# A two-layer trunk on one core: early splits of the weight blocks behind each norm, a shorter norm chain, a rebuilt opening and new ranks

## The chip, the core and the metric

The kernel runs on one core of a Trainium2 chip. PE (TensorE) multiplies, ACT (ScalarE) and DVE (VectorE) do the elementwise work, POOL (GpSimd) some fetches and stores, and SP (SyncE) issues most of the transfers from HBM. The metric is the device time of one execution in microseconds; the time before is the median of three runs, and one further execution was profiled.

## The reference, cut

```python
D_MODEL = 2048; SEQ = 256; DEPTH = 2; D_FF = 5120      # one sequence, f32
# layer 0: mixer = gated DeltaNet (16 q/k heads, 32 v heads of 128, chunks of 64)
# layer 1: mixer = sparse attention (16 heads of 128, an indexer picks the keys), bias by distance
for i in range(DEPTH):
    x = layer_norm(alpha * x + mixer_i(x), ln1_g[i], ln1_b[i])
    x = layer_norm(alpha * x + conv_glu(x), ln2_g[i], ln2_b[i])
    x = x + sigmoid(x @ ple_w_gate[i]) * (p[i] @ ple_w_proj[i])
...
def layer_norm(x, g, b):
    mu = jnp.mean(xf, -1, keepdims=True)
    var = jnp.mean(jnp.square(xf - mu), -1, keepdims=True)
    y = (xf - mu) * lax.rsqrt(var + LN_EPS) * g + b
```

So there are four norms: norm 1 and norm 2 in layer 0 (behind the mixer and behind the feed-forward part), norm 3 and norm 4 in layer 1.

## The kernel before

All 256 rows of x stay in the core (two tiles of 128 rows, called a = 0 and 1), and the weights, some 500 MB, are streamed once. A weight block is 128 x 1024 numbers, 512 KB. `weigh` makes three steps of it: a load into one of three `raw` buffers, issued by SP (L349); a rounded copy `hi`, by ACT (L354) or, when pressed, by DVE (L358); and `lo`, the rest `raw - hi`, by DVE (L362). hi and lo have three buffers each. PE then multiplies x, split in the same way and transposed (`xT`), by both: in wide blocks (mm_ps: L306 by hi, 512 columns, and L303 by lo, 256 columns) or in column blocks of 512 outputs (b_ps: L316 and L317 by hi, L319 by lo). A `column` is the chain of blocks that fills one pair of PSUM tiles; at its end `done` takes it on.

At a norm, `project` adds the product to x by a residual operation on DVE (L217 or, unscaled, L215) and takes statistics (L1102). `norm` aggregates them (L1111), works out 1/sqrt by `newton` (L628 to L643), subtracts and scales x (L1124 on DVE for a = 0, L1126 on ACT for a = 1, which needs `nm` of L1115), has PE transpose it (n_ps, L1134), applies gain and bias (L1145 on ACT, L1149 on DVE) and splits it (cast L1158, rest L1161, both on DVE). While that chain runs, PE has only the two `fill` columns of p @ ple_w_proj (b_ps<-hi,pT), two blocks in all. The first products behind a norm need the first pair of xT and the first blocks' hi and lo.

The order of the work is made ahead of time by a planner: `add(engine, estimated us, what, dependencies, rank=...)` puts a step on an engine, and of the steps that could start, the one of least rank goes first. `RANK` holds the numbers: 'later' is the rank of a weight split that is not yet pressing, 'near' says how many blocks ahead it becomes pressing. Each engine, and each queue of transfers, then runs its list in order.

The opening loads ident by SP (L197), x in quarters (L266), and the first blocks of gdn_w_in; POOL issues five small constants (L248 to L252). Layer 0's mixer ends with eight groups: `mixes(5)` and `mixes(6)` multiply groups' outputs by gdn_w_o and add them to x, and `project` does it for group 7 (O[7], written by L979, ready when `od[7]` is). In layer 1's mixer, `fetch` loads the bias tiles by POOL (L1408). The last columns of the second layer go through `ple`: sigmoid on ACT (L1296), product and sum on DVE (L1298, L1300), and the output's transfer (L1303).

## Time and profile before

| | us |
|---|---|
| median of 3 runs | 2812.58 (2812.26 to 2814.76) |
| the profiled execution, its own time | 2815.96 |
| its span | 2814.1 |
| PE busy in the span | 2787.2 |
| DVE busy | 1883.9 |
| ACT busy | 1420.6 |

The span is the time from the first to the last instruction of the profiled execution; 1.86 us of its time lie around it. Busy times are sums over an engine's instructions; weight loads of PE run beside its products. An idle time in the views is put down to the event that ended it.

### The profile page before, as it was taken

The numbers are of one execution on the slowest core, as the hardware profiler recorded it, in microseconds if no ns is written. First come the engines' busy times: TensorE is split into PE (matmuls) and PEld (weight loads), VectorE is DVE, ScalarE is ACT, GpSimd is POOL, SyncE is SP. The second block draws the span as 40 slices with busy tenths as digits, with TensorE's granted clock in tenths as the row PEclk, the third lists the DMA queues.
The fourth block names the chain that finished last, engine by engine and source line by source line (L and its number), as shares of the span: only waits on it lengthen the run. The fifth ranks groups of instructions, "written<-read, shape, count | busy, mean of one in ns | idle before, by whom it ended". The sixth has DMA issues, their size and how long they took to land.

```text
span 2814.1 us, 39810 instructions
## 1 busy us (share of the span) xinstructions
PE 2787.2 (99%) x15054; PEld 2405.8 (85%) x15054; DVE 1883.9 (67%) x2931; ACT 1420.6 (50%) x2260; POOL 115.1 (4%) x191
## 2 busy tenths in 40 slices
...
GB/s 190 216 187 162 180 153 189 169 155 166 159 139 167 206 206 210 207 197 189 187 200 191 197 208 174 183 152 159 191 173 195 199 196 189 198 192 186 198 181 190
DMA packets 402272, 519.62 MB, mean 185 GB/s; under 512 B 19708, under 2 KB 288384, under 8 KB 402080
## 3 DMA queue, kind: packets, MB, share of 16 engines
...
## 4 chain that ended last, share of the span: by engine, by line
PE 93%; DVE 3%; DMA 3%; ACT 1%; issue 0%; SPq 0%; ACTq 0%; DVEq 0%
PE mm_ps L306 32%; PE mm_ps L303 17%; PE b_ps L317 12%; PE b_ps L316 12%; PE b_ps L319 12%; PE s_ps L834 2%; DMA raw<-in_gdn_w_in 2%; DVE lo L362 1%; DMA raw<-in_dsa_w_in 1%; PE o_ps L940 1%; PE w_ps L834 0%; PE ss_ps L661 0%; PE sc_ps L1384 0%; PE lg_ps L1470 0%; ACT hi L354 0%
## 5 line engine op out<-in xcount | busy, mean ns | idle before, releaser
L362 DVE TENSOR_TENSOR lo<-raw,hi 128x1024 fp32r<-128x1024 f32 x925 | 1129.4, 1223 | 724.6 <-ACT hi L354 716.3
L354 ACT ACTIVATE hi<-raw 128x1024 fp32r<-128x1024 f32 (+1 forms) x878 | 928.6, 1058 | 1166.7 <-PE mm_ps L306 535.7
L306 PE MATMUL mm_ps<-xT,hi 128*128 128x512 f32 (+1 forms) x4176 | 1028.8, 395 | 6.3 <-ACT hi L354 3.7
L306 PEld LDWEIGHTS mm_ps<-xT,hi 128*128 128x128 f32 (+1 forms) x4176 | 764.5, 189 | 154.9 <-ACT hi L354 4.3
L303 PEld LDWEIGHTS mm_ps<-xT,lo 128*128 128x128 f32 (+1 forms) x4176 | 537.3, 191 | 22.4 <-DVE lo L362 2.0
L303 PE MATMUL mm_ps<-xT,lo 128*128 128x256 f32 (+1 forms) x4176 | 549.6, 284 | 1.4 <-DVE lo L362 1.3
L316 PE MATMUL b_ps<-hi,xT 128*128 128x512 f32 (+1 forms) x704 | 273.3, 390 | 3.9 <-DVE xT L1158 2.6
L317 PE MATMUL b_ps<-hi,xT 128*128 128x512 f32 (+1 forms) x704 | 270.7, 387 | 0.4 <-DVE xT L1161 0.4
L316 PE MATMUL b_ps<-hi,hTA 128*128 128x512 f32 x512 | 199.4, 389 | 0.0
L317 PE MATMUL b_ps<-hi,hTA 128*128 128x512 f32 x512 | 199.4, 389 | 0.0
L319 PE MATMUL b_ps<-lo,xT 128*128 128x512 f32 (+1 forms) x704 | 187.4, 387 | 0.0
L316 PEld LDWEIGHTS b_ps<-hi,xT 128*128 128x128 f32 x704 | 132.8, 189 | 30.3 <-DVE xT L1158 3.1
L317 PEld LDWEIGHTS b_ps<-hi,xT 128*128 128x128 f32 x704 | 132.9, 189 | 26.4 <-DVE xT L1161 1.1
L319 PEld LDWEIGHTS b_ps<-lo,xT 128*128 128x128 f32 x704 | 129.6, 189 | 25.8
L319 PE MATMUL b_ps<-lo,hTA 128*128 128x512 f32 x512 | 136.9, 390 | 0.0
L317 PEld LDWEIGHTS b_ps<-hi,hTA 128*128 128x128 f32 x512 | 96.2, 188 | 19.9
L316 PEld LDWEIGHTS b_ps<-hi,hTA 128*128 128x128 f32 x512 | 96.2, 188 | 19.9
L319 PEld LDWEIGHTS b_ps<-lo,hTA 128*128 128x128 f32 x512 | 96.2, 188 | 19.9
L316 PE MATMUL b_ps<-hi,oT 128*128 128x512 f32 x256 | 102.9, 402 | 0.0
L317 PE MATMUL b_ps<-hi,oT 128*128 128x512 f32 x256 | 100.3, 392 | 0.0
L445 DVE SCALAR_TENSOR_TENSOR ac<-pd,cw,ac 128x256 f32<-128x256 f32 x192 | 90.7, 481 | 3.7 <-ACT ac L442 0.4
L1228 DVE SCALAR_TENSOR_TENSOR fac<-fpd,fcw,fac 128x256 f32<-128x256 f32 x160 | 73.7, 481 | 2.8
(287 smaller groups left out, 2333.9 us busy)
## 6 DMA issues: line engine op xcount, KB each, us to landing
...
raw<-in_ffn_w_gate SPq DMA_DIRECT2D x160, 512.0 KB, 4.5
raw<-in_ffn_w_up SPq DMA_DIRECT2D x160, 512.0 KB, 3.7
raw<-in_ffn_w_down SPq DMA_DIRECT2D x160, 512.0 KB, 4.0
...
```

Of the source, the lines that this page charges most:

```text
L303: nc.tensor.matmul(ps[o][:m, S:], lo[:, k, o * P:o * P + m], xk[:, 0], start=False, stop=e)
L306: nc.tensor.matmul(ps[o][:m], hi[:, k, o * P:o * P + m], xk.rearrange("p a b -> p (a b)"), start=s, stop=e)
L316: nc.tensor.matmul(ps[o][:, c], xh, hi[:, k, c], start=s, stop=False)
L317: nc.tensor.matmul(ps[o][:, c], xl, hi[:, k, c], start=False, stop=False)
L319: nc.tensor.matmul(ps[o][:, c], xh, lo[:, k, c], start=False, stop=e and c.stop == n)
L354: nc.scalar.activation(hi, box["raw"], AF.Copy)
L362: nc.vector.tensor_tensor(lo, box["raw"], box["hi"].bitcast(F32), op=ALU.subtract)
L445: nc.vector.scalar_tensor_tensor(box["ac"], pd[:, k:k + S], wt[:, k:k + 1], box["ac"], op0=ALU.mult, op1=ALU.add)
L834: nc.tensor.matmul(ps[:, h], lhs[:, h], rhs[:, h], start=True, stop=True)
L940: nc.tensor.matmul(ps[:, h], qd()[:, a, h], u()[:, a, h], start=not a, stop=True)
L1228: x = add(V, 0.48, lambda k=k, pd=pd, ac=ac, m=m: nc.vector.scalar_tensor_tensor(ac(), pd()[:, k:k + S], w["taps"](k, m), ac(), op0=ALU.mu ...
```

## The change

The change has six parts.

- **Opening.** ident is loaded by ACT's queue, and the five constants by SP, behind the third to sixth weight block (`settings`). The first quarter of x and the first two weight blocks are loaded and split in halves. Six products of zeros (`spin`) run on PE before the first real product.
- **Early splits.** `weigh` takes a `home`: blocks that are used behind a norm are loaded into the right half of `pw` and split into tiles that hold nothing at that time (hTB at norm 1; xT2 and hTB at norm 3; hTA at norms 2 and 4), while the last column of the projection runs: two fill blocks at norm 1, the two fills and the first four blocks behind the norm at the others. `after` puts the next five blocks' splits behind certain pairs of the norm.
- **Norm chain.** `newton` has 8 operations in place of 10, `nm` is made beside the chain, the first x piece of a = 1 is DVE's. The last column of a projection ends in three pieces (512, 256 and 256 wide), and `close` interleaves the last two blocks so that a = 0 ends first. `weave` takes the first gate and up blocks by halves.
- **Groups 6 and 7** are projected together, in one PSUM chain of 8 (`project` of gdn_w_o[24 * P:]); group 7's own steps get rank `last`, and its root is taken apart for each a.
- **Tail.** The last column of `ple` ends in pieces of 512, 256 and 256.
- **Queues and ranks.** The bias tiles are loaded by SP at rank -1 behind weight loads; the numbers of `RANK` change.

The diff, cut to its core:

```diff
-            'later': 3.45,
-            'cast': 2,
+            'later': 2.2,
...
-            'hold': 0.9}
+            'hold': 0.05,
...
-        nc.sync.dma_start(out=self.ident, in_=t["cst"][:, C_IDENT:C_IDENT + P])
+        nc.scalar.dma_start(out=self.ident, in_=t["cst"][:, C_IDENT:C_IDENT + P])
...
+        def spin(n, begin=False, end=False):
+            if begin:
+                box1["ps"] = sps("bk", [S], "w_ps")
+            for _ in range(n):
+                nc.tensor.matmul(box1["ps"], pads[0][:, :P], pads[0][:, 3:], start=True, stop=True)
+
+        spun = add(E, 5.0, lambda: spin(5, True), take=["bk"], rank=-9)
...
+            d = [order[2]["load"]]
+
+            def one():
+                nc.sync.dma_start(out=cr, in_=t["gdn_conv_w"].rearrange("k (n c) -> n k c", c=P))
+
+            def two():
+                for i, k in enumerate(("gdn_dt_bias", "gdn_a_log")):
+                    nc.sync.dma_start(out=w[:, 256 + 32 * i:288 + 32 * i],
+                                      in_=bass.AP(tensor=t[k].tensor, offset=t[k].offset, ap=[[0, P], [1, 32]]))
+
+            def three():
+                nc.sync.dma_start(out=ng, in_=t["gdn_norm_g"].rearrange("(p o) -> p o", o=1))
+                nc.sync.dma_start(out=self.cst, in_=t["cst"][:, P:])
+            a = add(Q, 0.4, one, behind=d, rank=2.2, bus=0.6, tail=2.0)
+            b = add(Q, 0.8, two, behind=[order[4]["load"]], rank=4.2, bus=0.2, tail=2.0)
+            return a, add(Q, 0.8, three, behind=[order[5]["load"]], rank=6.2, bus=1.1, tail=2.0), b
...
+            n = 2 if not nb else 4
+            for j in range(0, 4, n):
+                parts = []
+                k0 = 4 * nb + j
+                for a in range(2):
+                    def load(a=a, k0=k0):
+                        cs = slice(k0 * P, (k0 + n) * P)
+                        nc.sync.dma_start(out=self.x[:, a, cs], in_=t["x"][a * P:(a + 1) * P, cs])
...
+                    if a and not k0:
+                        add(E, 0.45, lambda: spin(1), [e], behind=[spun], give=["bk"], rank=0.5)
...
+                ends = [(0, slice(0, 512)), (1, slice(0, 256)), (1, slice(256, 512))] if split and k0 + nk == kt else None
...
+                raw = box["raw"] = (home(2).rearrange("p (k n) -> p k n", k=b["nk"]) if home else
+                                    self.wp.tile(shape, F32, tag="raw", name="raw"))
...
+                hi = box["hi"] = at_home(0) if home else self.hl.tile(shape, F32R, tag="hi", name="hi")
...
+            if i < 2:
+                h, l = [], []
+                for j in range(2):
+                    def load(j=j):
+                        (c0, n) = b["cols"]
+                        if not j:
...
+                    d = b["load"] = add(Q, 0.38, load, take=["raw"] * (not j), rank=i if i else j - 2.5, bus=0.9, tail=2.0,
+                                        behind=[d] if j else [last["load"]] if i else ())
+                    h.append(add(A, 0.63, high, [d], take=["hi"] * (not j), rank=0, behind=h[:j],
+                                 other=(V, 0.39, cast, lambda: 1)))
+                    l.append(add(V, 0.66, low, [h[j]], take=["lo"] * (not j), give=["raw"] * j, rank=0, behind=l[:j]))
...
+            if home is None:
+                behind, ahead = [*behind, *split[:1]], split[1:]
+            else:
+                ahead = ()
+            h = add(A, 0.2 + 0.86 * size, high, [d, *deps], take=["hi"] * (not home), rank=urgent, behind=behind,
                     other=(V, 0.1 + 0.6 * size, cast, lambda: R["cast"] if near() else 9))
-            l = add(V, 0.1 + 1.13 * size, low, [h], take=["lo"], give=["raw"], rank=urgent)
-            b["weights"] = dict(hi=h, lo=l)
+            l = add(V, 0.1 + 1.13 * size, low, [h], take=["lo"] * (not home), give=["raw"] * (not home), rank=urgent,
+                    behind=ahead)
...
+        def close(a, b):
+
+            weigh(a)
+            weigh(b)
+            ks, (one, *two) = range(2), b["ends"]
+            multiply(a, [(one, ks)], False)
+            multiply(b, [(one, ks)], False)
+            multiply(a, [((1, slice(0, 512)), ks)], True)
+            multiply(b, [(w, ks) for w in two], True)
+
+        def weave(a, b):
+
+            weigh(a)
+            weigh(b)
+            for j in (0, 2):
+                for one in (a, b):
+                    multiply(one, pieces(one, range(j, j + 2)), j == 2)
...
+        def after(blocks, pairs):
+
+            rest = [b for b in blocks if "weights" not in b]
+            for n, b in enumerate(rest[:5]):
+                k = R["after"] + n - R["free"]
+                weigh(b, behind=pairs[k][1:] if n >= R["free"] and k < 8 else ())
+
+        def run(blocks, soon=()):
+
+            for i, b in enumerate(blocks):
+                if i in soon:
+                    weigh(*soon[i]())
+                if "next" in b:
+                    return close(b, b["next"])
...
-            def step():
-                y, u, zz = box["y"], box["t"], z()
-                nc.vector.scalar_tensor_tensor(u, y, -0.5 / c, y, op0=ALU.mult, op1=ALU.mult)
-                nc.vector.tensor_tensor(u, u, zz, op=ALU.mult)
-                nc.vector.scalar_tensor_tensor(y, u, 1.5, y, op0=ALU.add, op1=ALU.mult)
...
+                nc.vector.tensor_scalar(yi, yi, -1.0, 1595561664.0, op0=ALU.mult, op1=ALU.add)
+
+            def more(ks):
+                y, u = box["y"], box["t"]
+                if ks[0][0] == 3:
+                    nc.vector.tensor_tensor(u, y, y, op=ALU.mult)
+                    nc.vector.tensor_tensor(u, u, z(), op=ALU.mult)
+                    box["p"] = z()
+                for k, c in ks:
+                    nc.vector.scalar_tensor_tensor(box["p"] if k else y, box["p"] if k < 3 else u, c, u if k else y,
+                                                   op0=ALU.add, op1=ALU.mult)
...
+            v_ = R["last"] if last else 2
...
+            for aa in ((0,), (1,)) if last else ((0, 1),):
...
+                    for i, (a, c, w) in enumerate(spans(nb)):
+                        xs_ = self.x[:, a, nb * 512 + c:nb * 512 + c + w]
+                        d = add(V, 0.14 + 0.275 * w / 256, lambda a=a, c=c, w=w, xs_=xs_: self.residual(
+                            xs_, state["ps"][a][:, c:c + w], scale), [task[i] if nb == 3 else task],
+                            give=["mm"] * (c + w == 512), rank=-2 if nb == 3 else 1)
...
+            minus = add(V, 0.16, lambda: nc.vector.scalar_tensor_tensor(
+                nm(), mv()[:, 1, 0:1], -1.0, r()[:, 1:2], op0=ALU.mult, op1=ALU.mult), [d], rank=-1.5)
...
+                        if a and k0 and k0 < R["even"]:
+                            before.append(add(A, 0.37 + 0.112 * n, lambda xa=xa: nc.scalar.activation(
+                                xa, xa, AF.Identity, scale=r()[:, 1:2], bias=nm()), [minus], rank=rank, behind=held))
+                        else:
+                            before.append(add(V, 0.14 + 0.13 * n, even, [d], rank=rank if k0 else -1.7, behind=held if a else ()))
...
-                        r[a, h] = add(G, 0.75, lambda a=a, h=h: nc.gpsimd.dma_start(
+                        r[a, h] = add(Q, 0.5, lambda a=a, h=h: nc.sync.dma_start(
...
+                            [opened, *stored], behind=[gates[a * 4 + h // 4]], rank=-1, bus=1.2 + 1.2 * a, tail=4.0)
...
-            run(mixes(6))
...
-                    c, st, stat = project(t["gdn_w_o"][28 * P:], 4, lambda k: O[7]()[:, k], lambda k0: od[7], 1.0, opened)
-                run(two(c[0], c[1]) if i else c[0] + c[1])
-                run(c[2])
-                run(c[3])
+                    c, st, stat = project(t["gdn_w_o"][24 * P:], 8, lambda k: O[6 + k // 4]()[:, k % 4],
+                                          lambda k: od[6 + k // 4], 1.0, opened)
...
+                homes = [(w["hB"], 0), (w["hB"], 1)]
+                blocks = [fills[0], fills[1]]
+                if i:
+                    blocks += [first[0][0], first[1][0], first[0][1], first[1][1]]
+                    homes = [(xb2, m) for m in range(4)] + homes
+                    deps = [opened, seq[-1]["task"]]
+                else:
+                    deps = [opened]
+                c = two(c[0], c[1]) + c[2] + c[3] if i else c[0][:2] + c[1][:2] + c[0][2:] + c[1][2:] + c[2] + c[3]
+                run(c, ahead_(range(16, 28, 2) if i else (8, 10, 12), blocks, homes, lambda n, deps=deps: deps))
...
+                blocks = [fills[2], fills[3], g[0][0], g[1][0], g[0][1], g[1][1]]
+                run(x, ahead_(range(6, 18, 2), blocks, [(w["hA"], m) for m in range(6)],
+                              lambda n, x=x: [x[2 * n + 1]["task"]]))
```

How the order of the engines changes, at three places. On DVE at norm 3, from the end of newton on, the order before; L362 is the lo of a weight block, L1158 and L1161 are the first pairs of x:

```order
L642 TENSOR_TENSOR rt_18615<-rt_18615,lz 128x2
L643 SCALAR_TENSOR_TENSOR rs_18614<-rt_18615,rs_18614 128x2
L1115 SCALAR_TENSOR_TENSOR lnm<-lmv,rs_18614 128x1
L1124 TENSOR_SCALAR x<-x,lmv,rs_18614 128x256 x2
L362 TENSOR_TENSOR lo<-raw,hi 128x1024 x3
L1158 CAST xT<-xb 128x2x256
L1161 TENSOR_TENSOR xT<-xb,xT 128x2x256
L1158 CAST xT<-xb 128x2x256
L1161 TENSOR_TENSOR xT<-xb,xT 128x2x256
L1124 TENSOR_SCALAR x<-x,lmv,rs_18614 128x512
L1149 TENSOR_SCALAR xb<-n_ps,gb_18159 128x256
```

and the order after (L1270 is x, L1257 nm, L1297 the gain and bias, L1308 and L1311 the split pairs, L406 the lo of a weight block):

```order
L758 SCALAR_TENSOR_TENSOR rs_18626<-lz,rs_18626 128x2
L1270 TENSOR_SCALAR x<-x,lmv,rs_18626 128x256 x2
L1257 SCALAR_TENSOR_TENSOR lnm<-lmv,rs_18626 128x1
L1270 TENSOR_SCALAR x<-x,lmv,rs_18626 128x256
L1270 TENSOR_SCALAR x<-x,lmv,rs_18626 128x512 x2
L1297 TENSOR_SCALAR xb<-n_ps,gb_18157 128x256
L1308 CAST xT<-xb 128x2x256
L1311 TENSOR_TENSOR xT<-xb,xT 128x2x256
L1297 TENSOR_SCALAR xb<-n_ps,gb_18157 128x256 x2
L1308 CAST xT<-xb 128x2x256
L1311 TENSOR_TENSOR xT<-xb,xT 128x2x256
```

The three lo splits that stood between x and its first pair have left this place; the next L406 stands eight rows further down.

On PE at norm 2, from the end of the second fill (hi and lo with pT) to the first product with xT, before:

```order
L316 MATMUL b_ps<-hi,pT 128x512
L317 MATMUL b_ps<-hi,pT 128x512
L319 MATMUL b_ps<-lo,pT 128x512 x4
L1134 MATMUL n_ps<-ident,x 128x128 x8
L316 MATMUL b_ps<-hi,xT 128x512
L317 MATMUL b_ps<-hi,xT 128x512
L316 MATMUL b_ps<-hi,xT 128x512
```

and after (hTA here holds the blocks that were split early, L1282 is the transpose):

```order
L351 MATMUL b_ps<-hTA,pT 128x512
L352 MATMUL b_ps<-hTA,pT 128x512
L1282 MATMUL n_ps<-ident,x 128x128 x4
L354 MATMUL b_ps<-hTA,pT 128x512 x4
L1282 MATMUL n_ps<-ident,x 128x128 x12
L351 MATMUL b_ps<-hTA,xT 128x512
L352 MATMUL b_ps<-hTA,xT 128x512
L351 MATMUL b_ps<-hTA,xT 128x512
```

The first four transposes have moved into the second fill, in front of its lo products, and twelve follow them before the first product, where eight stood behind the fill. At norm 1 all transposes still stand behind both fills.

On SP in the opening, before:

```order
L197 DMA ident<-in_cst 128x128
L266 DMA x<-in_x 128x512 x2
L349 DMA raw<-in_gdn_w_in 128x4x256 x2
L266 DMA x<-in_x 128x512 x2
L349 DMA raw<-in_gdn_w_in 128x4x256 x2
```

and after:

```order
L298 DMA x<-in_x 128x256 x2
L420 DMA raw<-in_gdn_w_in 128x2x256
L298 DMA x<-in_x 128x256 x2
L420 DMA raw<-in_gdn_w_in 128x2x256 x3
L298 DMA x<-in_x 128x512 x2
L393 DMA raw<-in_gdn_w_in 128x4x256
L273 DMA cr<-in_gdn_conv_w 64x4x128
```

ident has left the queue, x and the weights come in halves at first, and the first constant stands behind the third block.

## Rows read from the trace of the kernel before

**Rows 1.** The page's first part: busy time of each engine in us, its share of the span, and instructions.

```profile
PE 2787.2 (99%) x15054; PEld 2405.8 (85%) x15054; DVE 1883.9 (67%) x2931; ACT 1420.6 (50%) x2260; POOL 115.1 (4%) x191
```

**Rows 2.** The windows view of core 0, five stretches. The columns are: stretch, its length in us, busy us (and instructions) of PE, PE's weight loads, DVE, ACT and POOL, the granted clock of PE as a share of full speed, the busy share of the DMA engines, GB/s.

```profile
0.00:41.50 41.50, 31.46 (x164) 26.28 (x165) 18.41 (x22) 16.25 (x22) 5.05 (x13) 1.00 0.75 211
41.50:200.00 158.50, 155.51 (x879) 134.30 (x878) 133.06 (x275) 100.95 (x198) 14.88 (x25) 1.00 0.70 199
200.00:850.00 650.00, 650.00 (x3765) 570.65 (x3764) 485.57 (x846) 349.80 (x692) 30.03 (x52) 1.00 0.57 163
...
1700.00:2024.00 324.00, 324.00 (x1784) 281.71 (x1783) 210.29 (x379) 156.43 (x253) 34.19 (x44) 1.00 0.56 172
2024.00:2052.00 28.00, 25.37 (x130) 21.03 (x130) 22.02 (x44) 17.53 (x28) 0.00 (x0) 0.94 0.42 132
```

**Rows 3.** The view of waits, of PE: line of the waiting instruction, what ended the wait, us in total, times, longest.

```profile
PE t_ps L273 <- DMA x<-in_x: 5.6, 1, 5.6
PE mm_ps L306 <- ACT hi L354: 3.7, 2, 3.2
PE b_ps L316 <- DVE xT L1158: 2.6, 2, 1.3
PE mm_ps L306 <- DVE xT L1161: 2.4, 2, 2.0
...
PE mm_ps L303 <- DVE lo L362: 1.3, 2, 1.0
```

**Rows 4.** The chain of work that ended last, two of its pieces from a stretch of gate and up projections: start, us, what, and how many instructions.

```profile
1055.80 3.65 PE mm_ps L306 x16
1059.45 1.91 PE mm_ps L303 x16
```

**Rows 5.** The timeline of PE around the four norms (norm 1 at 888, 2 at 1566, 3 at 2029, 4 at 2708 us): start, us, engine, line, operation, output<-input, shapes, how many, and in brackets the idle time before with what ended it. b_ps<-hi,pT at the head of a norm is the first fill product; mm_ps and b_ps<-hi,xT are products of the normed x; n_ps are its transposes.

```profile
888.68 0.50 PE L316 MATMUL b_ps<-hi,pT 128*128 128x512 f32 x1
...
897.21 1.18 PE L306 MATMUL mm_ps<-xT,hi 128*128 128x512 f32 x4
...
1566.01 0.40 PE L316 MATMUL b_ps<-hi,pT 128*128 128x512 f32 x1
...
1578.20 1.03 PE L1134 MATMUL n_ps<-ident,x 128*128 128x128 f32 x8
...
2029.49 0.40 PE L316 MATMUL b_ps<-hi,pT 128*128 128x512 f32 x1
...
2039.03 3.44 PE L306 MATMUL mm_ps<-xT,hi 128*128 128x512 f32 x8 [2.02 <-DVE xT L1161]
2042.31 1.04 PE L1134 MATMUL n_ps<-ident,x 128*128 128x128 f32 x8
...
2707.97 0.40 PE L316 MATMUL b_ps<-hi,pT 128*128 128x512 f32 x1
...
2721.72 1.03 PE L1134 MATMUL n_ps<-ident,x 128*128 128x128 f32 x8
```

**Rows 6.** The timeline of DVE behind norm 3's statistics.

```profile
2031.44 0.17 DVE L1113 TENSOR_SCALAR lz<-lmv 128x2 f32<-128x2 f32 x1
...
2033.50 0.73 DVE L1124 TENSOR_SCALAR x<-x,lmv,rs 128x256 f32<-128x256 f32 x2
2034.15 3.49 DVE L362 TENSOR_TENSOR lo<-raw,hi 128x1024 fp32r<-128x1024 f32 x3
2037.82 0.43 DVE L1158 CAST xT<-xb 128x512 fp32r<-128x512 f32 x1 [0.18 <-ACT xb L1145]
2038.28 0.69 DVE L1161 TENSOR_TENSOR xT<-xb,xT 128x512 fp32r<-128x512 f32 x1
```

**Rows 7.** The timeline of ACT there.

```profile
2035.33 1.08 ACT L1126 ACTIVATE x<-x,lnm,rs 128x256 f32<-128x256 f32 x2
```

**Rows 8.** The windows view at norms 2 and 3, columns as in rows 2.

```profile
2040.00:2042.00 2.00, 2.00 (x6) 1.56 (x5) 0.50 (x2) 0.00 (x0) 0.00 (x0) 0.52 0.87 293
...
1574.00:1576.00 2.00, 0.95 (x3) 0.58 (x4) 1.73 (x5) 2.00 (x5) 0.00 (x0) 1.00 0.97 314
```

**Rows 9.** The timeline of all engines in the opening: SP's issue of ident's load (us is the issue), and ACT's first hi.

```profile
0.74 0.38 SPq L197 DMA_DIRECT2D ident<-in_cst  x1
...
10.02 1.06 ACT L354 ACTIVATE hi<-raw 128x1024 fp32r<-128x1024 f32 x1 [1.46 <-DMA raw<-in_gdn_w_in]
```

**Rows 10.** The timeline of PE in the opening.

```profile
5.62 2.31 PE L273 MATMUL t_ps<-ident,x 128*128 128x128 f32 x8 [5.62 <-DMA x<-in_x]
11.13 2.07 PE L306 MATMUL mm_ps<-xT,hi 128*128 128x512 f32 x4 [3.21 <-ACT hi L354]
...
22.43 1.22 PE L303 MATMUL mm_ps<-xT,lo 128*128 128x256 f32 x8 [1.01 <-DVE lo L362]
```

**Rows 11.** The DMA view of the first 20 us: GB/s in 40 equal slices of 0.5 us.

```profile
GB/s 0 0 0 91 110 219 180 141 225 160 92 20 33 221 307 320 338 387 234 248 287 299 291 355 377 365 363 352 320 346 354 361 352 381 361 367 369 205 55 20
```

**Rows 12.** The timeline of all engines at the end of the span.

```profile
2808.96 0.60 ACT L1296 ACTIVATE xb<-b_ps 128x512 f32<-128x512 f32 x1 [0.76 <-PE b_ps L319]
...
2810.32 0.69 DVE L1300 TENSOR_TENSOR x<-x,xb 128x512 f32<-128x512 f32 x1
```

**Rows 13.** The timeline behind group 7 of layer 0's mixer: DVE's last instruction on its output oT, and PE's first product that reads it.

```profile
862.06 0.74 DVE L979 SCALAR_TENSOR_TENSOR oT<-ot_ps,ng,oT 128x512 fp32r<-128x512 f32 x1
...
865.66 0.39 PE L316 MATMUL b_ps<-hi,oT 128*128 128x512 f32 x1
```

353 lines of the change are left out of this document (205 added, 148 removed).

## The prediction

> **What bounds the kernel now.** I read the totals first, then a table of stretches, then the waits of PE, then single stretches. The totals [rows 1] show PE busy for 2787.2 us, 99% of the span, with DVE at 67% and ACT at 50%. A table [rows 2] says where the rest is: 200 to 850 us is full to the last digit, while the opening (31.46 busy of 41.5) and the stretch of a norm (25.37 of 28 from 2024 us) are not; from 41.5 to 200 us PE lacks 3.0 us with DVE busy for 133.06 of 158.5. PE has the same products to do after the change, so only these holes can be gained, and new ones can open. The waits of PE [rows 3] name the largest: the first x transfer (5.6), two waits for the hi part of a weight block (3.7), the split, transposed x behind the norms (2.6 and 2.4) and two waits for a lo (1.3, of which 1.0 is the opening's).
>
> The holes are larger than their waits, because matmuls beside them run slowly. I size each as elapsed time less its matmuls at the steady pace: 0.228 us for a 512-wide product (16 take 3.65 [rows 4]), 0.233 in the fills, and about half for a 256-wide one or a transpose.
>
> **The change part by part.**
>
> *Norms.* From the end T of a projection's last product, where the first fill product starts, to a point at which PE runs on at full pace [rows 5]: norm 2 takes from 1566.01 to 1578.20, 12.2 us, and holds 24 fill products (5.6), 8 transposes (0.9) and 12 products (2.7): 9.2, so 3.0 lost. Norm 3, 2029.49 to 2042.31, is 12.8 us for 24 fills, 8 transposes and 8 products (8.3): 4.5 lost. Norm 4, 2707.97 to 2721.72, is 13.75 for the same 9.2 as norm 2: 4.55 lost. Norm 1 takes 8.5 us from 888.68 to its first product at 897.21, for 5.6 of fills and 1.8 of transposes: 1.1 lost, and some 0.6 in small waits behind it (the rest of the 2.4 and 1.3 of [rows 3]).
>
> Why it waits stands in norm 3. DVE ends the second residual and its statistics, does 12 tiny steps from 2031.44 at about 0.2 us a step, the first two x pieces from 2033.50, and then goes for 3.49 us into three lo splits of weight blocks (2034.15 to 2037.64), so the cast of the first x pair starts only at 2037.82 and its lo ends at 2038.97 [rows 6]. ACT's own x piece comes at 2035.33 [rows 7], behind a hi cast of such a block. After the change those splits are done while the projection still runs. By the new order of DVE (fences in the section on the change) no weight split stands between the Newton steps and the first x pairs, 9 tiny steps stand there in place of 12, and the first two x pieces are both DVE's.
>
> Priced from T: the last statistics now cover 256 columns and stand behind 256-wide residuals, so by T+1.1, aggregate 1.3, 9 steps x 0.2 to 3.1, two x pieces (0.73) to 3.85; before, ACT's x pieces began at T+5.8. The first four transposes stand inside the second fill (the PE fences), at T+4.6 to 5.1; put (0.55), cast 0.43 and lo 0.69 follow, with the handovers, to about T+7.4. PE is then free at 5.6 of fills + 16 transposes x 0.11 = T+7.4. So 0 to 0.5 us is left at norms 2 to 4; I take 0.3, and gain 2.7 + 4.2 + 4.25. At norm 1 both fills still stand ahead of all transposes in the new order, so the first product is near T+7.9 against 8.5: gain 0.6 and about 0.5 of the later waits, 1.1. **Norms: 12.2; bounds 5.5 to 14.** The low bound is half of the three, if one of ACT's evictions or the transposes comes in late. The cover of the splits is the projection in front: six blocks cost 6 x 1.06 of ACT and 6 x 1.22 of DVE in stretches where PE is full and DVE busy for about two thirds (22.02 of 28 [rows 2] with the norm in it); nothing if spread, and a late projection block if not (rival B).
>
> Half of norms 3 and 4 is clock: from 2040 to 2042 PE was granted 0.52 of full speed, the lower of its two levels (1.2 of 2.4 GHz) [rows 8], and norm 3's products stand 0.43 us apart (8 in 3.44 [rows 5]); norm 4's stretch is as much too long; behind a like idle norm 2 reads 1.00 [rows 8]. The Trainium skill ("TensorE: Matmul & The Clock Gate", Part 1) says the default state is throttled and activity releases it, and that how many matmuls run slowly varies from run to run. By it the runs without a profile need not have paid there, and the sum would be some 3 us smaller (8 products at 0.2 extra, twice); by the row it is as above.
>
> *Opening.* The first transpose starts at 5.62 and the first product at 11.13, after the hi of a whole 512 KB block that landed at 10.0 [rows 9]; the products then stand 0.5 apart (4 in 2.07), and one wait of 1.0 follows at 22.43 [rows 10]. The stretch to 41.5 us holds 31.46 busy [rows 2], of which about 5 are slow pace: about 15 are lost. After: four x pieces of 128 KB, half a block (256 KB) and ident (64 KB) must land: 832 KB, while the halves behind them share the engines. The traffic row [rows 11], summed, has that much by 7.3 us and 1.6 MB by 10. So the half block is there at 7.3 to 9.6, its cast takes 0.4 to 0.6, and the first product is at 7.8 to 10.2: gain 0.9 to 3.3, I take 2.5. The waits behind it lose half their block: 0.5 to 1.5, I take 1.0. Five dummy products in the dead time may bring the full level earlier: 0 to 3.4 (the slow stretch's whole loss); the granted clock reads full there while the matmuls are slow, so I take 0.5. **Opening: 4; bounds 1.5 to 8.** The constants' five transfers move from POOL to SP behind the weights; each takes SP about the 0.38 us of ident's issue [rows 9] and puts off the block behind it by that, which the three raw buffers hide; if they don't, 5 x 0.38 = 1.9, inside the bounds. ident itself goes to ACT's queue, idle then. The Trainium skill ("DMA: Bandwidth & Descriptors", Rules for kernel authors) advises at least 1 MiB for each DMA for full bandwidth. That speaks against the halves: by it the gain here would go to the lower bound, 1.5.
>
> *Tail.* Behind the last matmul come a sigmoid of 0.60, a product and a sum of 0.69 each, then the output [rows 12], to the span's end at 2814.1. With a 256-wide last piece they are about 0.41, 0.42 and 0.42: 0.7 less, and half as many bytes: **0.9; 0.5 to 1.3.**
>
> *The rest.* The two hi waits of [rows 3] hold 3.2 of the opening; the other 0.5 is where layer 1's mixer starts, and may go: **0.5; 0 to 1.** The 256-wide column ends (about 0.012 a product, 6 products at six places) and one dummy between transposes cost **-0.7.** Joining the last two groups' projections saves 8 residual adds on DVE, which PE does not see, but asks for group 7's output 10.9 us (4 blocks x 2.72) earlier; its last part was ready at 862.80, PE used it at 865.66 [rows 13]: 2.8 of slack. In the new order its first transposes follow its last output products directly, where 52 rows of other PE work stood between. I take **-0.5; -6 to 0.** The bias loads, moved from POOL to SP behind the weights, are eight more issues on a queue that has one block to issue in each 2.8 us (8 x 0.228 + 8 x 0.12); PE is full from 1700 to 2024 [rows 2]: 0, and if all eight hold up a block, 3.0 (8 x 0.38). New rank numbers elsewhere: PE is full there, 0; -8 to +3 (the 3.0 of 41.5 to 200).
>
> **Sum:** 12.2 + 4 + 0.9 + 0.5 - 0.7 - 0.5 = 16.4. The profiled execution took 2815.96 (span 2814.1 and 1.86 around), so 2799.6; the median of the runs shown is 3.4 below the profiled one, so **2796.2**.
>
> **The rivals.** A: half the norms' gain and the low end of the opening, because another late step takes over (ACT's evictions between transposes and x, or the second halves landing). 6.1 + 1.5 + 0.2: 7.8, 2804.8. For it: the four norms' chains are serial and x is not ready before T+7.4 by my own sum. Against: each step's duration is in the trace.
>
> B: group 7's output comes late, or the six early splits delay a projection block. With the old chain PE waits 10.9 - 2.8 = 8.1: 16.4 + 0.5 - 8.1 = 8.8 gives 2803.8; with A's halves 2812.4. For it: group 7's chain runs on DVE beside a lo of 1.2 us for each block, and PE takes its matmuls in order. Against: the chain stands earlier in the order.
>
> C, the other side: the ranks. From 41.5 to 200 us DVE is 84% busy [rows 2]; splits of weights now yield to other DVE work more often, and a lo that comes late stops PE at once. There are 57 blocks of 2.8 us in that stretch; if each third waits one lo (1.2 us, the 3.49 for three of [rows 6]), 23 us are lost and it ends at 2819.2. It decides from 16.4 + 5.6, that is 22 us. Against: PE idles 3.0 there now.
>
> D: the change does not do what it says: x is held by the projection's end, not by the splits. Then opening and tail and the rest count, 4.2: 2808.4. The 3.49 of lo ahead of the cast speaks against it.
>
> **How the numbers follow.** Forecast 0.62, A 0.16, B 0.09, C 0.08, D 0.05. The range takes the forecast's own bounds (2789 to 2801), A, B and D, and leaves C and the far ends of the opening: 2789 to 2808, about 8 in 10. About 0.2% (5.6 us) is what a measurement can tell from no change, so faster is below 2807.0: forecast, A, most of B: 0.82. Same: D and the rest of B: 0.10. Slower, above 2818.2: 0.08.
>
> **What would show it.** Right: between the Newton steps and the first casts of x no lo on DVE; first product behind norms 2 to 4 at T+7.2 to 8 and at 0.23 us pace; first product of the opening at 8 to 10; tail 0.5 to 1.3 us shorter. Wrong: PE waits for od-derived tiles near 860, PE waits for lo in 41.5 to 200, or a stall at the norms that ends on an ACT row in place of a DVE one.

## The result, and the profile after

The changed kernel took 2800.22 us (median of 4 runs, 2797.45 to 2801.43) against 2812.78 for the kernel before (4 runs): a ratio of 0.995, 95% interval [0.9937, 0.9962], 12.6 us faster. Forecast was 2796.2, range 2789 to 2808. Its profiled execution took 2797.45, the fastest of the four; that of before, 2815.96, is slower than any of before's four. One of the later runs of the kernel before took 14930 us and is left out of every number below.

The waits of PE after (engine, line, what ended the wait; us, times, longest). Against [rows 3], the first transfer of x, the hi waits and all waits behind norms 2 to 4 are gone or small; what is left is one at norm 1 (1.8), two in the opening (1.5, 0.8), and three between 70 and 230 us (0.6, 1.1, 1.1); w_ps is the dummies' own start (pd is the input of the convolution in layer 0's mixer, written by DVE; ot_ps is the transpose of a group's output there):

```profile
PE mm_ps L341 <- DVE xT L1311: 1.8, 1, 1.8
PE t_ps L305 <- DVE xT L311: 1.5, 1, 1.5
PE w_ps L265 <- DVE pd L255: 1.2, 1, 1.2
PE mm_ps L341 <- DVE pd L548: 1.1, 1, 1.1
PE ot_ps L1098 <- DVE n L938: 1.1, 1, 1.1
PE t_ps L305 <- DMA x<-in_x: 0.8, 1, 0.8
PE b_ps L351 <- ACT hi L398: 0.6, 1, 0.6
```

The windows after, columns as in [rows 2]. The opening stretch holds 37.99 us of PE work where it held 31.46, 5.24 of it the dummies; the stretch of norm 3 is full (27.92 of 28, where 25.37 was), and 200 to 850 has lost 1.15 us of its fullness (the ot wait that ends at 227.7):

```profile
0.00:41.50 41.50, 37.99 (x210) 31.47 (x211) 26.46 (x41) 18.97 (x31) 2.08 (x7) 1.00 0.84 242
41.50:200.00 158.50, 156.82 (x884) 136.13 (x883) 132.03 (x272) 106.40 (x202) 16.89 (x29) 1.00 0.68 196
200.00:850.00 650.00, 648.85 (x3754) 568.67 (x3753) 478.62 (x826) 356.98 (x697) 28.18 (x50) 1.00 0.57 163
2014.00:2042.00 28.00, 27.92 (x163) 23.82 (x162) 21.77 (x47) 13.81 (x23) 0.00 (x0) 1.00 0.22 66
```

The timeline of PE after, at norm 1 and norm 3 (compare [rows 5]). Norm 3's first product comes at 2027.43, 7.9 us behind T (2019.58), with no wait, and its first products start 0.23 to 0.34 us apart; the first four transposes stand inside the fill. At norm 1 PE waits 1.84 us behind its transposes:

```profile
888.70 1.03 PE L1282 MATMUL n_ps<-ident,x 128*128 128x128 f32 x8
891.57 1.21 PE L341 MATMUL mm_ps<-xT,hi 128*128 128x512 f32 x4 [1.84 <-DVE xT L1311]
...
2019.58 0.39 PE L351 MATMUL b_ps<-xT,pT 128*128 128x512 f32 x1
...
2024.23 0.78 PE L1282 MATMUL n_ps<-ident,x 128*128 128x128 f32 x4
2024.77 1.18 PE L354 MATMUL b_ps<-xT,pT 128*128 128x512 f32 x4
2025.78 1.57 PE L1282 MATMUL n_ps<-ident,x 128*128 128x128 f32 x12
2027.43 1.20 PE L341 MATMUL mm_ps<-xT,xT 128*128 128x512 f32 x4
```

The timeline of DVE after, at norm 3 (compare [rows 6]): from the last tiny step to x and on to the cast of the first pair stands no lo. The cast starts 6.65 us behind T, where it was 8.33 (2037.82 - 2029.49):

```profile
2023.47 0.16 DVE L758 SCALAR_TENSOR_TENSOR rs<-lz,rs 128x2 f32<-128x2 f32 x1
2023.67 0.74 DVE L1270 TENSOR_SCALAR x<-x,lmv,rs 128x256 f32<-128x256 f32 x2
2024.33 0.15 DVE L1257 SCALAR_TENSOR_TENSOR lnm<-lmv,rs 128x1 f32<-128x1 f32 x1
...
2026.23 0.43 DVE L1308 CAST xT<-xb 128x512 fp32r<-128x512 f32 x1
```

The timeline of PE in the opening after (compare [rows 10]). The trace counts each product of zeros twice; ten of these twelve dummies run until 5.8, two between the transposes and the next wait. The second transposes wait for DVE; the first product comes at 8.99 in place of 11.13, and the first four take 1.17 us, not 2.07:

```profile
1.19 4.64 PE L265 MATMUL w_ps<-pd 128*128 128x256 f32 x10 [1.19 <-DVE pd L255]
...
8.46 0.77 PE L305 MATMUL t_ps<-ident,x 128*128 128x128 f32 x4 [1.53 <-DVE xT L311]
8.99 1.17 PE L341 MATMUL mm_ps<-xT,hi 128*128 128x512 f32 x4
10.93 0.63 PE L305 MATMUL t_ps<-ident,x 128*128 128x128 f32 x4 [0.78 <-DMA x<-in_x]
```

The end of the span after (all engines; compare [rows 12]). The operations are as short as forecast (0.42), but both sigmoids (L1445 x2) start only behind the very last matmul, so the last sum ends 2.1 us behind that matmul's end as it did before:

```profile
2790.45 0.28 PE L354 MATMUL b_ps<-lo,xT 128*128 128x256 f32 x1
2790.77 0.66 ACT L1445 ACTIVATE xb<-b_ps 128x256 f32<-128x256 f32 x2 [2.19 <-PE b_ps L354]
...
2792.44 0.42 DVE L1450 TENSOR_TENSOR x<-x,xb 128x256 f32<-128x256 f32 x1
```

**Where the time went** is told by the starts of four matmuls, the first fill product of each norm (T1 to T4), and of the first product with oT, in the profile of each kernel:

| kernel | first oT | T1 | T1 to T2 | T2 to T3 | T3 to T4 | T4 to end |
|---|---|---|---|---|---|---|
| before | 247.66 | 888.68 | 677.33 | 463.48 | 678.48 | 106.13 |
| after | 242.71 | 883.21 | 676.82 | 459.55 | 674.31 | 101.78 |
| again | 243.43 | 883.93 | 676.79 | 459.56 | 674.33 | 101.79 |
| mute_spin | 245.94 | 886.44 | 676.83 | 459.53 | 674.33 | 101.86 |
| pool_bias | 248.27 | 888.77 | 676.82 | 461.68 | 674.33 | 101.81 |
| norm1_order | 243.98 | 884.48 | 675.71 | 459.52 | 674.35 | 101.78 |
| before_busy | 249.06 | 890.08 | 677.27 | 462.80 | 677.24 | 104.61 |
| late_splits | 243.95 | 884.45 | 677.65 | 465.69 | 676.37 | 103.24 |
| long_chain | 255.70 | 900.19 | 676.78 | 461.20 | 677.55 | 103.46 |
| old_opening | 257.82 | 901.07 | 678.41 | 459.60 | 674.33 | 101.93 |
| old_ranks | 250.02 | 891.45 | 676.94 | 459.73 | 674.35 | 101.85 |
| no_spin | 246.55 | 887.05 | 676.81 | 459.54 | 674.33 | 101.86 |
| two_projects | 245.07 | 885.57 | 681.47 | 459.51 | 674.33 | 101.80 |
| better | 244.54 | 885.03 | 675.79 | 459.54 | 674.33 | 101.79 |

Two things are to be seen. From T1 on, kernels with the same order agree within 0.1 us a stretch, and after is 12.96 us shorter than before (0.51 + 3.93 + 4.17 + 4.35). Ahead of T1 the same order gives different times: after, again, norm1_order and pool_bias have one order there on every engine (late_splits and two_projects have it too, up to 840 us), and T1 between 883.21 and 888.77, all of it ahead of the first oT product (from there to T1 all six take 640.5). Five of the six lie within 2.4 us; pool_bias is the sixth.

### The profile page after: what moved, and what is told of

It is laid out like the page before. It is cut to its first block, busy times and chain, and to the rows that moved or that the text cites. A ratio compares the mean times of both kernels' runs of the same rounds, so it can differ in the third digit from the quotient of the medians.

```text
span 2795.7 us, 39873 instructions
## 1 busy us (share of the span) xinstructions
PE 2782.5 (100%) x15102; PEld 2404.6 (86%) x15102; DVE 1885.8 (67%) x2939; ACT 1426.9 (51%) x2261; POOL 105.1 (4%) x177
## 4 chain that ended last, share of the span: by engine, by line
PE 97%; DVE 2%; DMA 1%; issue 0%; SPq 0%; ACT 0%; DVEq 0%; ACTq 0%
PE mm_ps L341 34%; PE mm_ps L338 17%; PE b_ps L351 13%; PE b_ps L354 13%; PE b_ps L352 13%; PE s_ps L951 2%; DMA raw<-in_gdn_w_in 1%; PE o_ps L1059 1%; PE w_ps L951 0%; DVE lo L406 0%; PE n_ps L1282 0%; PE ss_ps L778 0%; PE sc_ps L1535 0%; PE lg_ps L1621 0%; PE o_ps L1058 0%; PE l_ps L855 0%
## 5 line engine op out<-in xcount | busy, mean ns | idle before, releaser
L406 DVE TENSOR_TENSOR lo<-raw,hi 128x1024 fp32r<-128x1024 f32 (+1 forms) x903 | 1104.3, 1224 | 689.4 <-ACT hi L398 681.0
L398 ACT ACTIVATE hi<-raw 128x1024 fp32r<-128x1024 f32 x869 | 919.2, 1058 | 1141.3 <-PE mm_ps L341 522.3
L341 PE MATMUL mm_ps<-xT,hi 128*128 128x512 f32 (+1 forms) x4144 | 1016.3, 393 | 2.9 <-DVE xT L1311 1.8
L341 PEld LDWEIGHTS mm_ps<-xT,hi 128*128 128x128 f32 (+1 forms) x4144 | 756.4, 188 | 149.5 <-DVE xT L1311 2.1
L338 PEld LDWEIGHTS mm_ps<-xT,lo 128*128 128x128 f32 (+1 forms) x4144 | 531.7, 191 | 20.0
L351 PE MATMUL b_ps<-hi,xT 128*128 128x512 f32 (+2 forms) x678 | 260.3, 386 | 0.6 <-ACT hi L398 0.6
L352 PE MATMUL b_ps<-hi,xT 128*128 128x512 f32 (+2 forms) x678 | 257.9, 383 | 0.0
L354 PE MATMUL b_ps<-lo,xT 128*128 128x512 f32 (+2 forms) x678 | 180.6, 384 | 0.0
L351 PEld LDWEIGHTS b_ps<-hi,xT 128*128 128x128 f32 x678 | 127.5, 188 | 25.7 <-ACT hi L398 1.0
L352 PEld LDWEIGHTS b_ps<-hi,xT 128*128 128x128 f32 x678 | 127.6, 188 | 24.1
L351 PE MATMUL b_ps<-hi,oT 128*128 128x512 f32 (+1 forms) x258 | 103.5, 401 | 0.0
L352 PE MATMUL b_ps<-hi,oT 128*128 128x512 f32 (+1 forms) x258 | 100.6, 390 | 0.0
```

Source lines behind the costliest of these rows:

```text
L338: nc.tensor.matmul(ps[o][:m, S:], lo[:, k, o * P:o * P + m], xk[:, 0], start=False, stop=e)
L341: nc.tensor.matmul(ps[o][:m], hi[:, k, o * P:o * P + m], xk.rearrange("p a b -> p (a b)"), start=s, stop=e)
L351: nc.tensor.matmul(ps[o][:, c], xh, hi[:, k, c], start=s, stop=False)
L352: nc.tensor.matmul(ps[o][:, c], xl, hi[:, k, c], start=False, stop=False)
L354: nc.tensor.matmul(ps[o][:, c], xh, lo[:, k, c], start=False, stop=e and c.stop == n)
L398: nc.scalar.activation(hi, box["raw"], AF.Copy)
```

## The experiments

Each kernel is the changed one with one edit, but for before_busy. Times are medians with the ratio to the kernel before, which ran beside them: 2813.9 (median of 20 runs) for again, no_spin, late_splits and before_busy; 2813.02 (23) for long_chain, old_opening, old_ranks and better; 2814.73 (9) for mute_spin, pool_bias, two_projects and norm1_order. These three groups ran on three chips, so times of two groups are compared by what each gains on its own kernel before.

**again**: no edit.

> The changed kernel once more, for the spread of its runs. Theory 1 (the clock in the opening differs from run to run): runs lie between 2797 and 2802 us, those near 2797.5 with a mean granted clock of 1.000 and those near 2801 with 0.999, and a profiled run above 2799 shows products about 0.43 us apart in the opening's first 8 products, while norms 2 to 4 have their first product at T+7.5 to T+7.9 and 0.23 us pace. Rival (the clock falls at the norms): such a run shows the slow products behind a norm. Second rival (no clock in it): the spread is in transfers, and the first product of the opening moves by 2 us or more.

2799.38 (2798.18 to 2801.02), 0.9947 [0.9935, 0.996]. The spread is as expected, but the mean granted clock is 0.999 in all five runs and sorts none of them, and T1 came out within 0.8 us of that of the first profile, which can't tell the theories apart. The profile of pool_bias, which has the same order ahead of T1, does: its T1 is 5.6 us later. At 73 us PE waits for the hi of a block whose transfer is late (0.58 us in after, 2.06 there), and then the granted clock falls to 0.63 and 0.52 until 84 us (timeline of PE, first after, then pool_bias, and the windows view of pool_bias; columns as in [rows 2]):

```profile
73.71 0.50 PE L351 MATMUL b_ps<-hi,xT 128*128 128x512 f32 x1 [0.58 <-ACT hi L398]
```

```profile
76.17 0.50 PE L351 MATMUL b_ps<-hi,xT 128*128 128x512 f32 x1 [2.06 <-ACT hi L398]
```

```profile
8.00:12.00 4.00, 2.92 (x10) 2.27 (x11) 3.60 (x8) 1.93 (x4) 0.00 (x0) 0.60 0.98 304
...
76.00:80.00 4.00, 3.83 (x14) 3.22 (x14) 3.15 (x3) 3.97 (x13) 0.00 (x0) 0.63 0.65 215
80.00:84.00 4.00, 4.00 (x12) 3.31 (x13) 2.91 (x12) 4.00 (x13) 0.00 (x0) 0.52 0.96 303
```

Product by product, of the 5.6 us 1.0 is lost by 12 us, 1.5 in the longer wait at 73 us, and 3.1 while the clock is low behind it. ACT's hi waits there for its block's load, 2.29 us in after and 4.00 in pool_bias. So the spread is transfers and clock together; the first theory named only the opening's part (0.60 from 8 to 12 in that run), and the rival's place, the norms, shows 1.00.

**no_spin** and **mute_spin**: without the dummies; no_spin also takes their steps from the plan, and the opening's order moves.

```diff
-        spun = add(E, 5.0, lambda: spin(5, True), take=["bk"], rank=-9)
...
-                        add(E, 0.45, lambda: spin(1), [e], behind=[spun], give=["bk"], rank=0.5)
```

```diff
         def spin(n, begin=False, end=False):
+            return
```

> The changed kernel without its six dummy products. Theory 1: the dummies raise the clock before the first product in some runs or all; without them the opening's first 8 to 12 products stand 0.43 to 0.5 us apart in every run, and every run is near the slow ones of the changed kernel, 2801 to 2803 us, with little spread. Rival: the dummies do nothing, and the median is within 0.5 us of the changed kernel's.

> The changed kernel in its own order on every engine, but the six dummy products are not issued (no_spin also moved the order of the opening). Theory 1: the dummies hold the first transposes back (they start at 3.5 without, 5.2 to 5.6 with) and raise the clock: the first product comes at the same 8.5 to 9.2, held by DVE's xT, but products stand 0.43 to 0.5 us apart until about 15 us, the 50th product comes 2 to 3 us later than 21.3 to 21.7, and the median is 2801.5 to 2803. Rival (no_spin's 3 us came from its other order): within 1 us of the changed kernel.

no_spin: 2802.68 (2799.39 to 2805.89), 0.9959 [0.9945, 0.9973]. mute_spin: 2801.99 (2800.77 to 2806.65), 0.9958 [0.9946, 0.9971]. The first product of no_spin comes at 6.14, that of mute_spin at 10.08, where 8.5 to 9.2 was expected. In both the products are slow (timelines of PE, first no_spin):

```profile
6.14 2.06 PE L338 MATMUL mm_ps<-xT,hi 128*128 128x512 f32 x4
...
9.80 2.07 PE L338 MATMUL mm_ps<-xT,hi 128*128 128x512 f32 x4 [1.18 <-DVE xT L310]
```

```profile
9.31 1.12 PE L302 MATMUL t_ps<-ident,x 128*128 128x128 f32 x4 [4.58 <-DVE xT L308]
10.08 2.06 PE L338 MATMUL mm_ps<-xT,hi 128*128 128x512 f32 x4
...
12.64 1.90 PE L338 MATMUL mm_ps<-xT,hi 128*128 128x512 f32 x4
```

The 51st product (the 50th of the expectations, which count from 0) is at 22.40 in no_spin and 23.32 in mute_spin. In the six profiles that have the dummies and one order in the opening it is at 21.25 to 22.68 (after 21.25, again 21.71). mute_spin, which has that order too, is 0.6 to 2.1 us behind them; no_spin lies inside their spread. Against its own kernel before, no_spin gains 11.2 and mute_spin 12.7, where again gains 14.5 and the changed kernel in its first four runs 12.6. So the dummies are worth something between 0 and 3 us, which these few runs don't narrow. Their price, first transposes at 5.2 to 5.6 us in place of 3.6 (mute_spin), does not show in the first product: it comes at 8.69 to 9.84 with them.

**late_splits**: nothing is split ahead.

```diff
-                run(c, ahead_(range(16, 28, 2) if i else (8, 10, 12), blocks, homes, lambda n, deps=deps: deps))
+                run(c)
...
-                run(x, ahead_(range(6, 18, 2), blocks, [(w["hA"], m) for m in range(6)],
-                              lambda n, x=x: [x[2 * n + 1]["task"]]))
-                w["staged"] = [b["weights"]["lo"][0] for b in blocks]
+                run(x)
```

> The changed kernel with no block split ahead in dead tile parts: fills and first blocks go through the usual buffers. Theory: DVE has lo splits to make in front of or between the first pairs of x again, the first product behind norms 2 to 4 comes at T+8.5 to 9.5 in place of T+7.5 to 7.9 and PE waits 1.0 to 2.0 us there: 3 to 6 us slower than the changed kernel, 2803 to 2806. Rival (the shorter chain alone made the gain): at most 1 us slower, first product at T+8 or earlier.

2809.38 (2804.2 to 2813.75), 0.9982 [0.9973, 0.9991]. From T1 on it is 10.5 us longer (0.8, 6.1, 2.1, 1.5). The first products come at T+7.9 to 8.4, only 0.4 to 0.5 later; a lo stands ahead of the first pair again (timeline of DVE at norm 2), and at every norm PE waits 0.7 us for a lo. By the 200th product the four norms lose 0.7, 1.5, 1.8 and 1.5, 5.5 in all, as the theory had it (3 to 6). Of the other 5.0, 4.7 are at one place, 55 us behind T2: a wait for ACT's sigmoid that ends at 1619.59, and the low clock behind it. ACT's list had stood still for 2.71 us ahead of that sigmoid, for DVE's gain and bias on x (L1327), which stands between lo splits there. That this is an order of the planner which the edit brought, and not the late splits' own load on DVE, is not shown.

```profile
1567.69 1.22 DVE L406 TENSOR_TENSOR lo<-raw,hi 128x1024 fp32r<-128x1024 f32 x1
...
1569.28 0.43 DVE L1308 CAST xT<-xb 128x512 fp32r<-128x512 f32 x1
```

```profile
1619.59 0.50 PE L351 MATMUL b_ps<-hi,xT 128*128 128x512 f32 x1 [2.76 <-ACT xb L1445]
```

**long_chain**: newton and nm as before, every x piece of a = 1 on ACT.

```diff
-            minus = add(V, 0.16, lambda: nc.vector.scalar_tensor_tensor(
+            d = minus = add(V, 0.16, lambda: nc.vector.scalar_tensor_tensor(
...
-                        if a and k0 and k0 < R["even"]:
+                        if a:
```

> The changed kernel with the norm chain of before: ten operations in newton, nm in the chain, and every x piece of a = 1 by ACT; the early splits stay. Theory (at norms 2 to 4 the first pair of x is ready just when PE is free, so what the chain is longer by shows): 0.4 us of tiny steps and about 0.5 us for ACT's piece, so the first product at T+8.2 to T+8.8 in place of T+7.5 to 7.9, 0.7 to 1.0 us at each of four norms: 2.5 to 4 us slower, 2802 to 2804. Rival (the splits made all of the gain, the chain has slack): within 1 us of the changed kernel.

2820.63 (2818.46 to 2822.45), 1.0026 [1.0015, 1.0036], slower than before. From T1 on it is 6.5 us longer, 1.7, 3.2 and 1.7 at norms 2, 3 and 4, and nothing at norm 1: the chain has no slack at three norms. At norms 2 and 4 that is waits for xT alone; at norm 3, behind a wait of 2.0, the granted clock also fell to half. But 13 us more are lost ahead of the first oT, and 4.0 from there to T1: newton is also used by the groups of layer 0's mixer, the planner's order there moves, and long waits open (view of waits of PE):

```profile
PE mm_ps L341 <- DVE pd L548: 5.4, 2, 4.3
...
PE ot_ps L1103 <- DVE n L943: 3.3, 1, 3.3
```

**old_opening**: before's `quarter`, whole blocks, constants on POOL, ident on SP, no dummies.

```diff
-            if i < 2:
+            if False:
...
-        nc.scalar.dma_start(out=self.ident, in_=t["cst"][:, C_IDENT:C_IDENT + P])
+        nc.sync.dma_start(out=self.ident, in_=t["cst"][:, C_IDENT:C_IDENT + P])
```

> The changed kernel with the opening of before: whole quarters and blocks, constants by POOL, ident by SP, no dummies. Prediction's term: 4 us slower, 2803.5 to 2806. Theory now (the profiled runs show 5.5 us between the openings but lie at opposite ends of their kernels' runs; in the medians some 1 to 2 us): 2800.5 to 2802.5, with a spread of 4 us that comes from the first 250 us.

2817.12 (2814.47 to 2819.43), 1.0012 [1.0003, 1.0021]. Its 51st product is at 24.43, 1.8 to 3.2 us behind the changed kernel's. Some 12 us more are lost up to the first oT, with waits in the mixer (4.4 for pd, 3.9 for ot) and the low clock behind them, 2.8 from there to T1, and 1.6 at norm 1. That the new ranks bring these waits with this opening is argued, not shown. So the run does not measure the opening.

**old_ranks**: before's numbers for the keys that both have.

```diff
-            'later': 2.2,
+            'later': 3.45,
...
-            'solve1': 3.7,
+            'solve1': 5,
```

> The changed kernel with before's numbers in RANK for all keys that both have (but hold). Prediction's term: 0. Theory: PE is full outside the holes, so only the waits at 73, 170 and 226 us and the start of layer 1's mixer can move: within 2 us of the changed kernel. Rival C turned round (ranks decide when lo splits come): 5 us or more of new waits in 41 to 250 us, or behind the norms where lo splits then stand ahead of x again.

2807.05 (2803.98 to 2808.21), 0.9972 [0.9963, 0.9982]. From T1 on nothing changes (0.4 us in all); ahead of it 7.5 us are lost against again. Of these 2.6 are lost by 16 us, where the order is still that of again: the granted clock fell at 9.0 us in this run. Some 4 are lost at 166 to 200 us (timeline of PE), with the granted clock at half from 176 to 183:

```profile
177.08 0.80 PE L341 MATMUL mm_ps<-xT,hi 128*128 128x512 f32 x1 [3.34 <-DVE pd L548]
179.07 1.65 PE L341 MATMUL mm_ps<-xT,hi 128*128 128x512 f32 x3 [1.20 <-DVE pd L548]
```

The ranks matter, mainly in one place. Each of long_chain, old_opening and old_ranks undoes one part and loses more than the part was forecast to hold, which suggests that the numbers fit this opening and this newton together.

**before_busy**: the kernel before, with 3 or 4 dummy products behind the first transposes of norms 2 to 4.

```diff
+                if k0 == 2 and busy:
+                    def keep():
+                        ps = sps("bk", [S], "k_ps")
+                        for _ in range(busy):
+                            nc.tensor.matmul(ps, self.ident, self.cst[:, :S], start=True, stop=True)
+                    add(E, 0.46 * busy, keep, [x], take=["bk"], give=["bk"], rank=1)
```

> The kernel before with dummy products on PE in the idle time between the first transposes and the first product of norms 2 (3 dummies, about 1.4 us), 3 (4) and 4 (3), so that PE does not idle there. Theory 2 (the median of before does not hold the low clock of norms 3 and 4 that its profiled run showed): its profile shows a granted clock of 1.00 and 0.23 us pace behind all norms, and its median is within 1 us of before's. Rival (every run of before paid there): its median is 2.5 to 3.5 us below before's.

2810.4 (2808.84 to 2813.87), 0.9987 [0.9978, 0.9996]. The granted clock stays at 1.00 at norm 3 (windows view; in [rows 8] 0.52), and T2 to the end is 3.4 us shorter than in before, as the medians are (3.5). Of the 3.4, 1.2 and 1.5 are gained by the 200th product of norms 3 and 4; the other 0.7 is a wait of 0.52 at the start of layer 1's mixer that this profile lacks, with no dummy near. At norm 2 the dummies give nothing; before's clock had not fallen there. So the theory falls: the runs of before did pay the low clock at norms 3 and 4, some 2.8 us.

```profile
2040.00:2042.00 2.00, 2.00 (x10) 1.40 (x9) 1.15 (x2) 0.54 (x2) 0.00 (x0) 1.00 1.06 366
```

**pool_bias**: the bias tiles by POOL.

```diff
-                        r[a, h] = add(Q, 0.5, lambda a=a, h=h: nc.sync.dma_start(
+                        r[a, h] = add(G, 0.75, lambda a=a, h=h: nc.gpsimd.dma_start(
```

> The changed kernel with the bias tiles loaded by POOL as before. PE's and ACT's orders stay. Theory: the 1.3 us that the stretch between the 200th product behind norm 2 and norm 3 became shorter (404.3 in place of 405.6) is the start of layer 1's mixer, whose weight blocks no longer share the transfers with the bias tiles: with POOL that stretch is 405 to 406 and the whole 1 to 1.5 us slower. Rival (the gain there is from the other order of splits): stretch and time as in the changed kernel, within 0.3 and 1 us.

2803.48 (2799.98 to 2806.78), 0.9961 [0.9948, 0.9973]. T2 to T3 is 2.1 us longer, behind the 200th product, with two waits of PE for a hi (1.1 us) and slower products beside them; the rest of the difference is its slow start. In the changed kernel the move to SP is worth those 2.1.

```profile
1683.16 0.34 PE L351 MATMUL b_ps<-hi,xT 128*128 128x144 f32 x1 [0.64 <-ACT hi L398]
...
1686.52 2.12 PE L341 MATMUL mm_ps<-xT,hi 128*128 128x512 f32 x8 [0.46 <-ACT hi L398]
```

**two_projects**: groups 6 and 7 apart.

```diff
             run(mixes(5))
+            run(mixes(6))
...
-                    c, st, stat = project(t["gdn_w_o"][24 * P:], 8, lambda k: O[6 + k // 4]()[:, k % 4],
-                                          lambda k: od[6 + k // 4], 1.0, opened)
+                    c, st, stat = project(t["gdn_w_o"][28 * P:], 4, lambda k: O[7]()[:, k], lambda k0: od[7], 1.0, opened)
```

> The changed kernel with groups 6 and 7 projected apart, as before: eight residual adds more on DVE, and group 7's output needed 10.9 us later. Prediction's term: the joint form costs 0.5 us. Theory: PE doesn't see the adds, and in the changed kernel no wait stands between 230 us and norm 1: the stretch from the first oT product to norm 1 is 640.5 in both, and the times agree within 1 us. Rival (DVE is short there, and the adds delay lo splits): 2 us or more of PE waits between 840 and 890 us.

2803.62 (2802.57 to 2804.54), 0.996 [0.9946, 0.9974]. The stretch from the first oT to T1 is 640.50, as in the changed kernel: PE sees neither the adds nor the earlier need, so the joint form costs it nothing up to T1. But norm 1 is 4.6 us longer, since with half the columns' length two lo and older statistics stand on DVE in front of its chain:

```profile
887.35 2.34 DVE L406 TENSOR_TENSOR lo<-raw,hi 128x1024 fp32r<-128x1024 f32 x2
889.61 1.34 DVE L1241 BATCH_NORM_STATS2 st<-x 128x6 f32<-128x256 f32 x3
```

```profile
894.54 2.29 PE L1282 MATMUL n_ps<-ident,x 128*128 128x128 f32 x9 [3.21 <-DVE x L1270]
```

That time is of the edit's own order, and inconclusive on the DVE's relief.

**norm1_order** and **better**: at norm 1 the first transposes inside the second fill; better also keeps the second half's cast of the first block off DVE.

```diff
                 p_, turned = norm(st, stat, gb1)
+                if not i:
+                    late, early = fills[1]["tasks"][-1], turned[0]
+                    late.left += 1
+                    early.then.append((late, False))
```

```diff
-                                 other=(V, 0.39, cast, lambda: 1)))
+                                 other=(V, 0.39, cast, lambda: 1) if i or not j else None))
```

> The changed kernel with its own opening, and only at norm 1 the first transposes inside the second fill. All order ahead of norm 1 is the changed kernel's. Theory: the 200th product behind norm 1 at T+46.7 in place of T+47.7, 1 us faster: 2798.0 to 2799.4. Rival: the wait of 1.8 us moves on to gain and bias or to a lo, and nothing is gained.

> The changed kernel with two orders mended: DVE may not take the cast of the first block's second half (it stood ahead of the rest of xT and waited for the transfer), and at norm 1 the first transposes go into the second fill as at the other norms. Theory: norm 1's first product at T+7.5 in place of T+8.4 and no wait there (0.8 to 1.8 us), the opening's first product at 7 to 8 us in place of 9.0 to 9.2 (1 to 2 us): 2796 to 2798. Rival (another step is late next, the transfers in the opening and gain and bias at norm 1): 2799 or above.

norm1_order: 2797.96 (2797.28 to 2802.38), 0.9943 [0.993, 0.9955], the fastest here, though its interval overlaps that of the changed kernel. T1 to T2 is 1.1 us shorter; the wait of 1.84 is 0.41:

```profile
889.06 0.86 PE L1282 MATMUL n_ps<-ident,x 128*128 128x128 f32 x4
...
890.68 1.58 PE L1282 MATMUL n_ps<-ident,x 128*128 128x128 f32 x12
892.67 1.20 PE L341 MATMUL mm_ps<-xT,hi 128*128 128x512 f32 x4 [0.41 <-DVE xT L1311]
```

better: 2799.19 (2798.26 to 2802.28), 0.9952 [0.9939, 0.9966], as the rival had it. Norm 1 is as in norm1_order; the opening's first product comes at 7.71, but PE then waits 2.6 us for x, and the 51st product is at 21.80: in the opening the transfer is next.

```profile
PE t_ps L305 <- DMA x<-in_x: 2.6, 1, 2.6
```

## Why the prediction was right, step by step

**What bounds.** Of the 18.4 us between the two profiled spans 13.7 are idle time of PE. Its busy time fell by 4.7 although the dummies added 5.2, so some 10 us of PE's other busy time are gone as well. The forecast had sized the holes as larger than their waits, with slow matmuls beside them, and its reading of what bounds was right.

**Norms, forecast 12.2.** By the 200th product behind each T, 0.4, 2.6, 3.9 and 4.2 us were gained (1.1, 2.7, 4.2 and 4.25 forecast): 11.1. The first product at T+7.5 (norms 2 and 4) and T+7.9 (norm 3) is where the sum from rows put it. Norm 1 gave less: its first product, sized as T+7.9, came at T+8.36 behind a wait of 1.84 for xT, and norm1_order, with the transposes inside the fill, gets 1.1 more there. late_splits and long_chain show that both edits are needed: without the one 5.5 are lost by the 200th products, without the other 6.5.

**From T1 on, in all.** The forecast's terms there (12.2 + 0.9 + 0.5 - 0.7) come to 12.9, and 12.96 was measured. That agreement is partly luck: the norms gave 1.1 less and the tail 0.7 less, the start of layer 1's mixer gave 0.8 more, and the column ends' cost of 0.7 is not to be seen (outside the other terms the stretches from T1 on are 0.4 shorter, not 0.7 longer).

**The clock at the norms.** The forecast took the low clock from the profile's row. before_busy shows that the runs paid it: 2.8 us at norms 3 and 4 between the profiles, 3.5 between the medians. The row was right, though 2.8 of the 9.05 us lost at these two norms (4.5 and 4.55) is nearer a third than the half that the forecast put down to the clock. The Trainium skill ("TensorE: Matmul & The Clock Gate", Part 1) states, of a kernel's start, that the number of slow matmuls varies from run to run. By that rule, taken over to the norms, the sum would have come out some 3 us smaller, and these runs don't bear it out there.

**Opening, forecast 4.** In the profiles the term holds. The 51st product comes at 26.70 and 25.67 in the two profiles with before's opening (before and before_busy) and at 21.25 to 22.68 in the six with the changed one, 4.3 earlier in the mean, and T1 is 4.3 earlier too. The opening's edits brought the first product 1.3 to 2.4 us forward (2.5 forecast); the dummies are 0.6 to 2.1 by mute_spin's profile (0.5 forecast). No run takes the half transfers back alone, so their part is not measured. The stretch to 41.5 us moved 242 GB/s where it had moved 211 [rows 2]; but from 12 to 16 us, with the DMA engines full in both (share 1.09 and 1.07), it is 293 GB/s where it was 355. The Trainium skill ("DMA: Bandwidth & Descriptors", Rules for kernel authors) advises at least 1 MiB for each DMA for full bandwidth. The lower rate from 12 to 16 us agrees with it, though the constants move in that stretch too; the first product, at 8.99, stands ahead of it.

**From the profiled run to the median.** This is the step that was off. The forecast measured the opening's loss in a profiled run that is at the slow end of before's runs, and then took 3.4 off for the median as if that lay elsewhere: 2799.6 without that step, 2796.2 with it, 2800.22 measured. If the runs without a profile share the stretches from T1 on, the result's medians leave -0.4 for all that lies ahead of T1, where 3.5 was forecast (the opening's 4 and group 7's -0.5); the same sum leaves 1.6 in again, and 0.5 to 2.8 in pool_bias, late_splits, norm1_order and two_projects. That they share them is argued from the profiles, not shown. So the gain ahead of T1 lies between about 0 (medians) and 4.3 (profiles). What a median run of before has that its two profiles lack, which run meets the late transfer at 73 us, and why T1 of the changed kernel's first two profiles came out earliest, stays open.

**Tail, forecast 0.9:** 0.2, below its bounds. The last column's pieces were priced rightly, their order not: neither sigmoid starts before the last matmul, so two short pieces follow each other where one long piece was in flight.

**Bias loads, forecast 0 with a loss as bound, and the start of layer 1's mixer, forecast 0.5:** a gain. Behind norm 2's 200th product the stretch to T3 is 1.3 shorter than before, and pool_bias gives 2.1 back. For the bias loads the sign was wrong: issued by POOL, they cost two waits of PE for a hi there.

**Group 7, forecast -0.5:** 0; no wait between 230 us and T1.

**Ranks, forecast 0:** from T1 on right; in the mixer ahead of it the old numbers lose some 5 of the 7.5 us of old_ranks. That is rival C's place (41.5 to 200 us), but the other way round: with the old numbers PE waits there for pd (4.5), other work of DVE, and once for a hi (1.7), and for no lo. **A, B and D** did not come: no ACT row ends a wait at norms 2 to 4, group 7 holds nothing up, and the splits are needed.
